# Splitting each 128x1024 weight tile with one cast and one subtraction in a decoder layer

## The chip, the cores and the metric

The kernel runs on one core of one Trainium2 chip. The metric is device time in microseconds (us) of one execution of the whole layer, as the median of several runs; lower is better.

## The reference

One decoder layer over 512 tokens with model width 2048: two gated token mixers side by side (latent attention and forgetting attention, 16 heads each), an output projection, then a product-key retrieval over 16384 single-neuron experts (8 heads, 16 experts a head and token). All of it is float32.

```python
h = rms_norm(x, mix_norm_g)
proj = einsum('bsd,de->bse', h, w_in)           # q, kv latents, fox q/k/v, forget, gates
...                                             # two causal attentions, y_a and y_b
merged = concatenate([y_a, y_b]) * sigmoid(gates + b_gate)
x = x + einsum('bse,ed->bsd', merged, w_out)
h2 = rms_norm(x, ffn_norm_g)
q = einsum('td,de->te', h2, w_peer_q)           # then scores, top-k of keys, top-k of pairs, softmax
a = einsum('td,thkd->thk', h2, u[experts])
x = x + einsum('thk,thkd->td', gates * gelu(a), v[experts])
```

## The kernel before

Every large product is made of three matmuls. A float32 operand is split into a rounded part `hi` (type float32r) and the rest `lo`; `mm3` (line 121) adds hi x hi, hi x lo and lo x hi. For a weight, `load` (line 92) brings a raw tile of 128 partitions x 1024 columns (512 KB) from memory on SP's queue; `half` (line 99) splits one half of it: a cast of 512 columns on ScalarE into `whi` and a subtraction on VectorE, or on GpSimd where `eng` says so, into `wlo` (`split`, line 87). So each raw tile costs two casts and two subtractions, and a tile `whi` with its tile `wlo` is called a pair here. Half a weight tile is called a unit or a half, a whole tile a whole.

The pools: phase 1 has NRAW = 3 raw tiles and 3 half pairs. Inside `spare(n, m)` (line 586) there is a second ring of n raw tiles and m half pairs; `load` counts all loads in `nraw` and takes the second ring when `nraw % nbuf >= NRAW`, with `nbuf` = NRAW + n. The output projection runs under `spare(NRAW2, NSP2)` = `spare(2, 3)`, the experts under `spare(1)`, that is one raw tile and two half pairs more.

The stages, in the order of time:

- Phase 1, the mixers (to about 1440 us). `col_tile` makes one 128x512 tile of the input projection from two raw tiles of `w_in`; `mla_pair` and `mla_head` use `w_up`. Attention work lies between them. There are 178 loads of w_in and 32 of w_up.
- Phase 2, the output projection (to about 1882 us). `merge` weaves a list of main units (`out_units`, tokens 0 to 511 in four blocks for q = 0, three blocks for q = 1) with a list of side units: `out0_units` finishes the first 128 tokens, `query0_units` makes their expert queries. Each main unit is 12 or 9 matmuls of 512 columns, each side unit 3. The first 14 main units stand alone; after that about 3.6 side units follow each main one. Odd halves of side tiles are subtracted on GpSimd. A unit is prepared (loaded, split) one place ahead of its use (LOOK = 1). After the merged list, q = 2 and 3 run alone, each with four groups (c) of four wholes (u).
- Phase 3, the queries of the other 384 tokens (`w_pq`), subtracted on GpSimd, with the top-k on VectorE, then the first 16 units of the expert rows (`up_stream`). Gathers of expert rows for the first tokens run from here on: `half` counts units and issues a gather on GpSimd's queue for every 400/128 units, whose product is a VectorE instruction of 2048 columns.
- Phase 4, the gate matrix (to about 2305 us; its order is written out by hand for TensorE, VectorE, ScalarE and GpSimd), with expert units between, and then the experts: `down` (`vt`) and `up_stream` (`ut`) in turn, 352 columns a matmul.

Outside the hand-ordered parts a planner orders each engine's instructions with a model of their times, by program order where several are ready, and gives out a buffer when its earlier tile has been released by all that used it.

Of the kernel before, what the change touches and what calls it, by code (L numbers as in the profile page):

```python
# [9 lines left out]
F32R = mybir.dt.float32r  # L10
# [9 lines left out]
P = 128  # L20
# [37 lines left out]
RC = 8  # L58
HALF = 512
RAWS = 3  # L60
NRAW = 3
NRAW2 = 2
NSP2 = 3
NC = 80
NU = 400
LAG = 28
# [10 lines left out]
class Kern:  # L77
# [18 lines left out]
        self.nc.sync.dma_start(raw[:, :n], src)  # L96
        return j, raw

    def half(self, w, i, eng=None):
        j, raw = w  # L100
        hi = self.wsp[j].tile([P, HALF], F32R, name="whi")
        lo = self.wsp[j].tile([P, HALF], F32R, name="wlo")
        ins = self.split(hi, lo, raw[:, i * HALF:(i + 1) * HALF], eng)
        self.last = lo
        if self.gathered is not None and not self.paused:
            self.units += 1
            if self.gathered < GATHERS and self.gathered * NU < self.units * PH * TOPK:
                with self.tc.issue_after(ins.ins):
                    self.gather(self.gathered)
                    self.gathered += 1  # L110
        return hi, lo

    def weight(self, src, n=1024, eng=None):
        w = self.load(src, n)
        return [self.half(w, i, eng) for i in range(n // HALF)]

    def cols(self, w, i, n):
        j, i = divmod(i, HALF)
# [86 lines left out]
    def col_tile(self, c):  # L205
        ps = self.mm.tile([P, SEQ], F32, name="mm")
        k = 0
        for u in range(2):
            w = self.early.pop((c, u), None) or self.load(self.a["w_in"][c, :, u])
            w = [self.half(w, i) for i in range(2)]  # L210
            for kt in range(8):
                self.mm3(ps, self.cols(w, kt * P, P), (self.hh[:, k], self.hlo[:, k]), k == 0, k == KD - 1)
                k += 1
        return ps
# [368 lines left out]
        return stack.enter_context(self.pool(name=name, bufs=1, side="right"))  # L583

    @contextlib.contextmanager
    def spare(self, n, m=2):
        with self.pool(name="wraw2", bufs=n) as wr, self.pool(name="wsp2", bufs=m) as ws:
            self.wraw.append(wr)
            self.wsp.append(ws)
            self.nbuf = NRAW + n  # L590
            yield
            self.nbuf = NRAW
            self.wraw.pop()
            self.wsp.pop()
# [22 lines left out]
    def piece(self, src, i, st, eng, run):  # L617
        def prep():
            if i == 0:
                st["w"] = self.load(src)  # L620
            return self.half(st["w"], i, eng)
        return prep, run

    def merged_half(self, q, i):
# [50 lines left out]
    def out0_units(self):  # L675
        st = {}
        m0 = self.right(self.low, "m0")
        mh = m0.tile([P, 24, P], F32R, name="m0h")
        ml = m0.tile([P, 24, P], F32R, name="m0l")
        raw = self.right(self.top, "m0r").tile([P, 24, P], F32, name="m0r")  # L680

        def unit(w, c, q, u, k2):
            if c == 0 and (u, k2) == (0, 0):
                qs = slice(q * 8 - 8, q * 8)
                self.nc.sync.dma_start(raw[:, qs], self.mrg[q * 8:q * 8 + 8, :, 0:P].rearrange("h p t -> p h t"))
                for k in range(q * 8 - 8, q * 8, 4):
                    self.split(mh[:, k:k + 4], ml[:, k:k + 4], raw[:, k:k + 4])
                if q == 3:
                    self.top.close()
            if (q, u, k2) == (1, 0, 0):  # L690
                st["ps"] = self.pa.tile([P, SEQ], F32, name="pa")
            k = (q - 1) * 8 + 2 * u + k2
            self.mm3(st["ps"], (mh[:, k], ml[:, k]), w, k == 0, k == 23)
            if k == 23:
                self.residual(st["ps"], 0, c, True)
                if c == 3:
                    self.low.close()
                    self.rows = self.right(self.low, "rows").tile([P, 3, D], F32, name="rows")
                    self.keys0 = self.rows[:, 2].rearrange("p (a b) -> p a b", b=NKEY)

        return [self.piece(self.a["w_out"][q, c, u], k2, st, self.nc.gpsimd if k2 else None,
                           lambda w, c=c, q=q, u=u, k2=k2: unit(w, c, q, u, k2))
                for c in range(4) for q in range(1, 4) for u in range(4) for k2 in range(2)]

# [9 lines left out]
    def query0_units(self, tk):  # L714
        nc = self.nc
        v = {}
        self.vals0 = tk.tile([P, 2, PH, TOPK], F32, name="vals0")
        self.ids0 = tk.tile([P, 2, PH, TOPK], U32, name="ids0")
        st = {}

        def norm():
            pool = self.right(self.top, "q0")
            v["hT"] = pool.tile([P, 2, KD, P], F32R, name="hT")
            v["qn"] = pool.tile([P, D], F32, name="qn")
            y = self.inv_rms(tk, range(1), "n0")
            for c in range(4):
                cs = slice(c * 512, c * 512 + 512)
                nc.vector.scalar_tensor_tensor(out=self.h0[:, cs], in0=self.x1[0][:, cs], scalar=y, in1=self.h0[:, cs],
                                               op0=OP.mult, op1=OP.mult)

        def turn(c):
            tp = self.pa.tile([P, 4, P], F32, name="pa")
            for i in range(4):
                k = 4 * c + i
                nc.tensor.transpose(tp[:, i], self.h0[:, k * P:k * P + P], self.ident)
            hT = v["hT"]
            self.split(hT[:, 0, 4 * c:4 * c + 4], hT[:, 1, 4 * c:4 * c + 4], tp)

        def query(w, c, k):
            if k == 0:  # L740
                st["ps"] = self.pa.tile([P, SEQ], F32, name="pa")
            self.mm3(st["ps"], (v["hT"][:, 0, k], v["hT"][:, 1, k]), w, k == 0, k == KD - 1)
            if k == KD - 1:
                nc.scalar.copy(v["qn"][:, c * 512:c * 512 + 512], st["ps"])

        def score(c):
            es = slice(4 * c, 4 * c + 4)
            qn = v["qn"]
            qT = self.rows[:, 0].rearrange("p (k t) -> p k t", t=P)
            sc = self.rows[:, 1].rearrange("p (k t) -> p k t", t=P)  # L750
            tp = self.pa.tile([P, 4, P], F32, name="pa")
            for i in range(4):
                nc.tensor.transpose(tp[:, i], qn[:, (4 * c + i) * P:(4 * c + i + 1) * P], self.ident)
            nc.scalar.copy(qT[:, es], tp)
            sp = self.pa.tile([P, 4, P], F32, name="pa")
            for i in range(4):
                nc.tensor.matmul(sp[:, i], qT[:, 4 * c + i], self.keys0[:, 4 * c + i], start=True, stop=True)
            nc.scalar.copy(sc[:, es], sp)
            for e in range(4 * c, 4 * c + 4):
                self.topk16(tk, self.vals0[:, e % 2, e // 2], self.ids0[:, e % 2, e // 2], sc[:, e], NKEY)  # L760

        bare = lambda f, *v: (lambda: None, lambda w: f(*v))
        out = [bare(norm)] + [None] * WAIT + [bare(turn, c) for c in range(4)]
        for c in range(4):
            out += [self.piece(self.a["w_pq"][c, k // 2], k % 2, st, nc.gpsimd if k % 2 else None,
                               lambda w, c=c, k=k: query(w, c, k)) for k in range(KD)]
            if c:
                out.insert(len(out) - KD + 4, bare(score, c - 1))
        return out + [bare(score, 3)]
# [59 lines left out]
    def phase3(self, hp):  # L829
        nc, a = self.nc, self.a  # L830
# [6 lines left out]
        with self.pool(name="tk", bufs=2) as tk, \  # L837
# [20 lines left out]
            for c in range(4):  # L858
# [1 line left out]
                ids = tk.tile([P, 2, ND, 2, TOPK], U32, name="ids")  # L860
                ps = [qp.tile([P, 512], F32, name="acc")[:, :TQ] for _ in range(4)]
                for u in range(8):
                    w = self.load(a["w_pq"][c, u])
                    for k2 in range(2):
                        k = 2 * u + k2
                        self.paused = c == 0 and k < 12
                        wh, wl = self.half(w, k2, nc.gpsimd)
                        for i in range(4):
                            es = slice(i * P, i * P + P)
                            self.mm3(ps[i], (wh[:, es], wl[:, es]), (self.dh[:, k], self.dl[:, k]), k == 0, k == KD - 1)  # L870
# [140 lines left out]
    def up_stream(self, rs, eng):  # L1011
        todo = [(r, u, i) for r in rs for u in range(2) for i in range(2)]
        raw = {}

        def fetch(r, u, i):
            if i == 0:
                raw[0] = self.load(self.a["ut"][r, u])
            return self.half(raw[0], i, eng)

        nxt = fetch(*todo[0])  # L1020
        for j, (r, u, i) in enumerate(todo):
# [5 lines left out]
            wh, wl = nxt  # L1027
            if j + 1 < len(todo):
                nxt = fetch(*todo[j + 1])
            for kt in range(4):  # L1030
                k = 8 * u + 4 * i + kt
# [99 lines left out]
    def build(self):  # L1131
        tc = self.tc
        with self.pool(name="cst", bufs=1) as cp, self.pool(name="dram", bufs=1, space=DRAM) as dp:
# [2 lines left out]
            self.xs = dp.tile([TQ, D], F32, name="xs")  # L1136
            self.hx = dp.tile([NX, D], F32, name="hx")
            self.aa = cp.tile([P, PH * TOPK], F32, name="aa")
            with self.pool(name="wraw", bufs=NRAW) as wr, self.pool(name="wsp", bufs=3) as ws:
                self.wraw, self.wsp = [wr], [ws]  # L1140
                self.phase1()
                with self.pool(name="res", bufs=1, side="right") as res:
# [98 lines left out]
```

## Time and profile before

| | us |
|---|---|
| median of 3 runs | 4241.0 |
| lowest and highest | 4234.29, 4250.6 |
| profiled execution | 4234.56 |
| its span, first to last instruction | 4232.8 |
| TensorE busy | 4095.4 (97%) |
| VectorE busy | 3083.4 (73%) |
| ScalarE busy | 1875.5 (44%) |
| GpSimd busy | 989.8 (23%) |

In the profile PE is TensorE's matmuls, PEld its weight loads, DVE VectorE, ACT ScalarE, POOL GpSimd and SP the queue that issues the loads. A matmul's record is about twice as long as the time to the next one's start, since they overlap; so TensorE's pace is read from starts or counts, not from the length of a record. "idle before" is the time that the engine stood still ahead of a group's instructions, with what ended it.

### The profile page before, as it was taken

What the parts mean: (1) busy time and instruction counts of PE and PEld (TensorE: products, weight loads), DVE (VectorE), ACT (ScalarE), POOL (GpSimd) and SP (SyncE); (2) the same over time, 40 slices, a digit from 0 to 9 for tenths busy, and PEclk for the clock granted to TensorE, in tenths of its full rate; (3) what the DMA queues carried; (4) which work ended last, traced back from release to release, by engine and by line L of the source; (5) the groups of instructions that cost most, each with busy time, mean ns of one, the idle gap of its engine ahead of it and who ended that gap; (6) DMA issues with size and microseconds to landing.
All of it is one profiled execution on the core that took longest, in us unless ns stands there. A gap on an engine that the chain in (4) does not pass through costs nothing.

```text
span 4232.8 us, 61035 instructions
## 1 busy us (share of the span) xinstructions
PE 4095.4 (97%) x22599; PEld 3734.9 (88%) x22599; DVE 3083.4 (73%) x5031; ACT 1875.5 (44%) x3584; POOL 989.8 (23%) x772
## 2 busy tenths in 40 slices
PE   8999999999999999998778999999999999999999
PEld 6878888888888777788778999999999999999998
DVE  8656556556655556868999878887878888888864
ACT  4555455555555455433266333333333333333332
POOL 1111111111101044227777111111111222221100
PEclk9999999999999999999899999999999999999999
DMA  4222222222222477665447888889888888988864
GB/s 135 88 80 80 79 86 85 78 82 90 78 85 83 146 245 243 202 268 204 151 143 225 340 306 330 323 326 325 318 310 315 319 320 326 333 328 322 314 222 145
DMA packets 245419, 896.81 MB, mean 212 GB/s; under 512 B 22816, under 2 KB 74016, under 8 KB 200992
## 3 DMA queue, kind: packets, MB, share of 16 engines
q1 hardware_dynamic: 190624, 540.47, 37.5%
q0 software_dynamic: 46272, 336.61, 21.5%
q10 hardware_dynamic: 8224, 15.82, 1.2%
q8 instruction: 177, 2.90, 0.3%
q14 instruction: 122, 1.00, 0.1%
HBM read 853.73 MB, written 39.06 MB: 211 GB/s over the span
## 4 chain that ended last, share of the span: by engine, by line
PE 85%; DVE 9%; issue 2%; DMA 2%; ACT 1%; POOL 1%; ACTq 0%; SPq 0%; DVEq 0%; POOLq 0%
PE acc L124 10%; PE acc L126 9%; PE acc L125 9%; PE mm L124 9%; PE mm L125 9%; PE mm L126 9%; PE a L126 7%; PE a L124 7%; PE a L125 7%; PE S L271 2%; DVE o L985 1%; DVE o L986 1%; DVE rows L915 1%; DMA raw<-w_out 1%; PE T L292 1%
## 5 line engine op out<-in xcount | busy, mean ns | idle before, releaser
L89 ACT CAST whi<-raw 128x512 fp32r<-128x512 f32 x1788 | 1097.9, 621 | 1808.0 <-PE acc L125 650.0
L90 DVE TENSOR_TENSOR wlo<-raw,whi 128x512 fp32r<-128x512 f32 x1596 | 1112.7, 709 | 652.6 <-ACT whi L89 622.4
L125 PE MATMUL acc<-Wl,whi 128*128 128x352 f32 x2048 | 660.1, 323 | 0.0
L124 PE MATMUL acc<-Wh,whi 128*128 128x352 f32 x2048 | 659.1, 324 | 0.5 <-ACT whi L89 0.5
L124 PE MATMUL a<-dh,whi 128*128 128x352 f32 x2016 | 657.0, 326 | 0.5 <-ACT whi L89 0.5
L126 PE MATMUL a<-dh,wlo 128*128 128x352 f32 x2016 | 648.8, 325 | 8.5 <-POOL wlo L90 8.0
L125 PE MATMUL a<-dl,whi 128*128 128x352 f32 x2016 | 654.1, 324 | 0.0
L126 PE MATMUL acc<-Wh,wlo 128*128 128x352 f32 x2048 | 627.1, 324 | 1.5 <-DVE wlo L90 1.5
L124 PE MATMUL mm<-hh,whi 128*128 128x512 f32 x1424 | 565.2, 397 | 8.7 <-ACT hh L526 8.7
L125 PE MATMUL mm<-hl,whi 128*128 128x512 f32 x1424 | 564.2, 396 | 6.4 <-DVE hl L527 6.3
L126 PE MATMUL mm<-hh,wlo 128*128 128x512 f32 x1424 | 562.1, 395 | 0.0
L126 PEld LDWEIGHTS a<-dh,wlo 128*128 128x128 f32 x2016 | 378.1, 188 | 10.1 <-POOL wlo L90 8.8
L124 PEld LDWEIGHTS acc<-Wh,whi 128*128 128x128 f32 x2048 | 384.5, 188 | 2.3 <-ACT whi L89 1.0
L125 PEld LDWEIGHTS acc<-Wl,whi 128*128 128x128 f32 x2048 | 385.2, 188 | 0.0
L126 PEld LDWEIGHTS acc<-Wh,wlo 128*128 128x128 f32 x2048 | 379.1, 188 | 3.2 <-DVE wlo L90 3.0
L124 PEld LDWEIGHTS a<-dh,whi 128*128 128x128 f32 x2016 | 379.3, 188 | 1.0 <-ACT whi L89 1.0
L125 PEld LDWEIGHTS a<-dl,whi 128*128 128x128 f32 x2016 | 379.3, 188 | 0.0
L90 POOL TENSOR_TENSOR wlo<-raw,whi 128x512 fp32r<-128x512 f32 x192 | 281.4, 1477 | 289.6 <-ACT whi L89 281.8
L125 PEld LDWEIGHTS mm<-hl,whi 128*128 128x128 f32 x1424 | 268.8, 189 | 65.8 <-DVE hl L527 11.5
L124 PEld LDWEIGHTS mm<-hh,whi 128*128 128x128 f32 x1424 | 269.5, 189 | 62.6 <-ACT hh L526 8.7
L126 PEld LDWEIGHTS mm<-hh,wlo 128*128 128x128 f32 x1424 | 269.0, 189 | 54.5 <-issue 0.2
L915 DVE CUSTOM_DVE_ANT_0 rows<-rows,h 128x2048 f32<-128x2048 f32 x128 | 300.3, 2347 | 6.7 <-DMA rows<-u,eidx 6.7
(374 smaller groups left out, 6431.9 us busy)
## 6 DMA issues: line engine op xcount, KB each, us to landing
raw<-ut SPq DMA_DIRECT2D x256, 512.0 KB, 5.3
raw<-vt SPq DMA_DIRECT2D x256, 512.0 KB, 6.1
raw<-w_in SPq DMA_DIRECT2D x178, 512.0 KB, 3.7
raw<-w_out SPq DMA_DIRECT2D x112, 512.0 KB, 4.6
raw<-w_pq SPq DMA_DIRECT2D x64, 512.0 KB, 4.3
gd<-rows SPq DMA_DIRECT2D x22, 1024.0 KB, 5.8
G<-gd SPq DMA_DIRECT2D x15, 1408.0 KB, 9.8
raw<-w_up SPq DMA_DIRECT2D x24, 512.0 KB, 3.6
```

Source lines behind the costliest of these rows:

```text
L89: nc.scalar.copy(hi, src)
L90: return (eng or nc.vector).tensor_tensor(out=lo, in0=src, in1=hi.bitcast(F32), op=OP.subtract)
L124: nc.tensor.matmul(out, wh, xh, start=start, stop=False)
L125: nc.tensor.matmul(out, wh, xl, start=False, stop=False)
L126: nc.tensor.matmul(out, wl, xh, start=False, stop=stop)
L271: nc.tensor.matmul(ps[:, :w], q[:, tb], k[:, :w], start=first, stop=False)
L292: nc.tensor.transpose(tp[:, (i - j) * P:(i - j + 1) * P], Ps[i][:, j * P:j * P + P], self.ident)
L915: nc.vector.tensor_tensor_reduce(out=row, in0=row, in1=self.h0, scale=1.0, scalar=0.0, op0=OP.mult, op1=OP.add, accum_out=self.aa[:, k:k + 1])
L985: nc.vector.tensor_tensor(out=o1, in0=lists[:, 0, t0:t0 + 4, None].to_broadcast(bc), in1=it, op=OP.is_equal)
L986: nc.vector.tensor_tensor(out=o2, in0=lists[:, 1, t0:t0 + 4, None].to_broadcast(bc), in1=it, op=OP.is_equal)
```

## The change

`half` becomes `whole`: one pair of 1024 columns, one cast and one subtraction per raw tile. A tile of 512 columns uses half of a wide pair. Callers that split half by half take both halves from the first call. Where odd halves went to GpSimd, odd tiles do. The count of units for the gathers goes up by two per tile, and at most one gather is issued per call.

The pools, in columns of pairs: 3 x 512 become 2 x 1024 in the first ring; in the output projection's second ring 3 x 512 become 1 x 1024; in the experts' 2 x 512 become 1 x 1024. Raw tiles: 3 become 2 in the first ring; the second rings keep 2 and 1.

```diff
-NRAW = 3
+NRAW = 2
 NRAW2 = 2
-NSP2 = 3
+NSP2 = 1
...
-    def half(self, w, i, eng=None):
+    def whole(self, w, n=1024, eng=None):
         j, raw = w
-        hi = self.wsp[j].tile([P, HALF], F32R, name="whi")
-        lo = self.wsp[j].tile([P, HALF], F32R, name="wlo")
-        ins = self.split(hi, lo, raw[:, i * HALF:(i + 1) * HALF], eng)
+        hi = self.wsp[j].tile([P, 1024], F32R, name="whi")
+        lo = self.wsp[j].tile([P, 1024], F32R, name="wlo")
+        ins = self.split(hi[:, :n], lo[:, :n], raw[:, :n], eng)
         self.last = lo
         if self.gathered is not None and not self.paused:
-            self.units += 1
+            self.units += n // HALF
...
-        return hi, lo
+        return [(hi[:, i:i + HALF], lo[:, i:i + HALF]) for i in range(0, n, HALF)]
 
     def weight(self, src, n=1024, eng=None):
-        w = self.load(src, n)
-        return [self.half(w, i, eng) for i in range(n // HALF)]
+        return self.whole(self.load(src, n), n, eng)
...
-            w = [self.half(w, i) for i in range(2)]
+            w = self.whole(w)
...
-    def spare(self, n, m=2):
+    def spare(self, n, m=1):
...
     def piece(self, src, i, st, eng, run):
         def prep():
             if i == 0:
-                st["w"] = self.load(src)
-            return self.half(st["w"], i, eng)
+                st["w"] = self.weight(src, eng=eng)
+            return st["w"][i]
...
-        return [self.piece(self.a["w_out"][q, c, u], k2, st, self.nc.gpsimd if k2 else None,
+        return [self.piece(self.a["w_out"][q, c, u], k2, st, self.nc.gpsimd if u % 2 else None,
...
-            out += [self.piece(self.a["w_pq"][c, k // 2], k % 2, st, nc.gpsimd if k % 2 else None,
+            out += [self.piece(self.a["w_pq"][c, k // 2], k % 2, st, nc.gpsimd if k // 2 % 2 else None,
...
-                    w = self.load(a["w_pq"][c, u])
+                    self.paused = c == 0 and u < 6
+                    w = self.weight(a["w_pq"][c, u], eng=nc.gpsimd)
                     for k2 in range(2):
                         k = 2 * u + k2
-                        self.paused = c == 0 and k < 12
-                        wh, wl = self.half(w, k2, nc.gpsimd)
+                        wh, wl = w[k2]
...
             if i == 0:
-                raw[0] = self.load(self.a["ut"][r, u])
-            return self.half(raw[0], i, eng)
+                raw[0] = self.weight(self.a["ut"][r, u], eng=eng)
+            return raw[0][i]
...
-            with self.pool(name="wraw", bufs=NRAW) as wr, self.pool(name="wsp", bufs=3) as ws:
+            with self.pool(name="wraw", bufs=NRAW) as wr, self.pool(name="wsp", bufs=2) as ws:
```

## Rows read from the trace of the kernel before

**Rows 1.** The page's busy times: us, share of the span, instructions.
```profile
PE 4095.4 (97%) x22599; PEld 3734.9 (88%) x22599; DVE 3083.4 (73%) x5031; ACT 1875.5 (44%) x3584; POOL 989.8 (23%) x772
```

**Rows 2.** By stage: length, busy PE, PEld, DVE, ACT, POOL (count); clock, DMA share, GB/s.
```profile
25.00:1440.00 1415.00, 1408.54 (x6801) 1159.08 (x6800) 859.82 (x1610) 760.71 (x1508) 175.44 (x125) 0.99 0.27 85
...
1490.00:1745.00 255.00, 241.23 (x1032) 189.37 (x1031) 159.84 (x295) 137.88 (x250) 107.15 (x77) 0.99 0.75 245
1745.00:1882.00 137.00, 130.89 (x574) 106.24 (x572) 111.02 (x233) 48.77 (x96) 26.23 (x16) 1.00 0.65 240
1882.00:1940.00 58.00, 55.03 (x318) 52.83 (x319) 31.05 (x78) 22.30 (x43) 28.57 (x22) 0.94 0.50 173
1940.00:2130.00 190.00, 143.05 (x797) 138.87 (x795) 187.60 (x651) 51.08 (x101) 142.45 (x82) 0.87 0.49 168
2130.00:2305.00 175.00, 145.01 (x1044) 138.70 (x1045) 170.89 (x174) 117.42 (x298) 144.34 (x138) 0.98 0.58 172
2305.00:4200.00 1895.00, 1891.47 (x11669) 1884.25 (x11668) 1507.00 (x1908) 697.39 (x1222) 347.57 (x298) 1.00 0.85 311
```

**Rows 3.** Groups of instructions: shape and count, then busy us, mean ns, idle before.
```profile
L90 DVE TENSOR_TENSOR wlo<-raw,whi 128x512 fp32r<-128x512 f32 x1596 | 1112.7, 709 | 652.6 <-ACT whi L89 622.4 <-PE y L126 11.4 <-PE mm L125 4.3
L89 ACT CAST whi<-raw 128x512 fp32r<-128x512 f32 x1788 | 1097.9, 621 | 1808.0 <-PE acc L125 650.0 <-PE a L125 478.5 <-PE mm L125 315.4
...
L928 DVE SCALAR_TENSOR_TENSOR x<-rows,aa,x 128x2048 f32<-128x2048 f32 x128 | 300.3, 2346 | 0.0
...
L90 POOL TENSOR_TENSOR wlo<-raw,whi 128x512 fp32r<-128x512 f32 x192 | 281.4, 1477 | 289.6 <-ACT whi L89 281.8 <-PE acc L126 5.0 <-POOL wlo L90 1.9
...
L89 ACT CAST Wh<-w 128x352 fp32r<-128x352 f32 x128 | 61.8, 484 | 22.6 <-DVE w L1054 21.7 <-PE acc L126 0.5
```

**Rows 4.** 2305 to 4200 us: the casts' group, and raw's landing times.
```profile
L89 ACT CAST whi<-raw 128x512 fp32r<-128x512 f32 x971 | 600.7, 621 | 1170.6 <-PE acc L125 573.9 <-PE a L125 475.0 <-DMA raw<-vt 38.0
...
DMA to landing us min/median/max: 3.4/5.8/16.5
```

**Rows 5.** The chain that ended last, 1535 to 1625 us: start, us, what.
```profile
1585.59 6.64 DMA raw<-w_out
...
1597.05 6.20 DMA raw<-w_out
```

**Rows 6.** Timeline of PE: start, us, instruction; first and last of thirteen.
```profile
1584.70 0.40 PE L126 MATMUL pa<-whi,m0l 128*128 128x512 f32 x1
...
1587.51 0.39 PE L126 MATMUL pa<-whi,m0l 128*128 128x512 f32 x1
```

**Rows 7.** 1490 to 1745 us: subtractions' ns min/median/max, landing, VectorE's group.
```profile
L90 DVE TENSOR_TENSOR wlo<-raw,whi x131: 666/693/1794, 1489.9 to 1741.7; 128x512 fp32r<-128x512 f32 x131
L90 POOL TENSOR_TENSOR wlo<-raw,whi x77: 1262/1297/2078, 1491.5 to 1734.9; 128x512 fp32r<-128x512 f32 x77
...
DMA to landing us min/median/max: 3.4/4.4/8.4
...
L90 DVE TENSOR_TENSOR wlo<-raw,whi 128x512 fp32r<-128x512 f32 x131 | 111.3, 870 | 81.0 <-ACT whi L89 76.9 <-POOL wlo L90 3.7
```

**Rows 8.** Timeline of DVE and of POOL from 1593 us.
```profile
1593.95 4.76 DVE L90 TENSOR_TENSOR wlo<-raw,whi 128x512 fp32r<-128x512 f32 x3 [0.17 <-ACT whi L89]
...
1593.47 2.99 POOL L90 TENSOR_TENSOR wlo<-raw,whi 128x512 fp32r<-128x512 f32 x2 [3.01 <-ACT whi L89]
```

**Rows 9.** 1745 to 1882 us: the casts' waits, and the gather products' group.
```profile
ACT whi L89 <- PE acc L126: 67.5, 47, 3.5
...
L915 DVE CUSTOM_DVE_ANT_0 rows<-rows,h 128x2048 f32<-128x2048 f32 x12 | 27.4, 2286 | 0.7 <-DMA rows<-u,eidx 0.6
```

**Rows 10.** 1882 to 1960 us: GpSimd's groups.
```profile
L90 POOL TENSOR_TENSOR wlo<-raw,whi 128x512 fp32r<-128x512 f32 x29 | 43.2, 1501 | 35.3 <-ACT whi L89 30.1 <-PE acc L126 5.0
L913 POOL DMA_INDIRECT rows<-u,eidx x6 | 5.7, 958 | 0.9 <-DVE ids L778 0.2 <-PE acc L126 0.2
```

**Rows 11.** 25 to 1440 us: raw's landing times.
```profile
DMA to landing us min/median/max: 2.6/3.7/6.9
```

## The prediction, made before the changed kernel was timed

> **What bounds the kernel now.** I read the busy times first: TensorE is busy 97% of 4232.8 us, VectorE 73%, ScalarE 44% [rows 1]. That says only which engine to fear for, so the next view is busy time stage by stage [rows 2]. Up to 1440 us (mixers) TensorE idles 6.5 of 1415 us, from 2305 to 4200 us (expert matmuls) 3.5 of 1895. From 1940 to 2305 us VectorE is the full one (187.6 of 190, then 170.9 of 175) and TensorE waits for top-k and the gate matrix. Between them lies the output projection, 1490 to 1745 us, where TensorE idles 13.8 of 255 and no engine is full.
>
> Then the splits themselves [rows 3]: a cast of 512 columns takes 621 ns, a subtraction 709 ns on VectorE, 1477 ns on GpSimd. None of it is on the path where TensorE is full: in the expert stage the casts idled 573.9 and 475.0 us waiting for TensorE to give back a pair [rows 4]. So cheaper splits buy nothing there; what can change the time is how early a pair and a raw tile come free. The chain of waits shows where that is tight already: around 1590 us it runs through DMA waits of 6.64 and 6.20 us for w_out [rows 5].
>
> **The price of a wide split.** Cast: 484 ns at 352 columns, 621 at 512, so 0.86 ns a column and 621 + 512 x 0.86 = 1.06 us at 1024. VectorE: 709 ns at 512, 2346 at 2048 [rows 3], so 709 + 512 x 1.07 = 1.25 us. GpSimd has no wider row of this form: between 1.3 us (its median now, no gain from more columns counted) and 2 x 1.3 = 2.6 us [rows 7]; I take 2.5, near the upper end, because the work doubles. A whole on VectorE thus saves 1.24 - 1.06 = 0.18 us of ScalarE and 1.42 - 1.25 = 0.17 of VectorE, on engines that wait anyway, but its first matmul waits 1.06 + 1.25 = 2.31 us (GpSimd: 3.56) where the half's waited 1.3 (1.9).
>
> **Mixers, 25 to 1440 us.** Three half pairs become two whole pairs, three raw tiles two. A whole feeds 24 matmuls; at 0.234 us a 512-column matmul (twelve steps in 2.81 us [rows 6]) that is 5.6 us. A pair given back is split again in 2.3 us plus queueing, while TensorE has the other whole for 5.6. A raw tile is held for 3.7 us of landing [rows 11] plus 2.3, and two serve 11.2 us of TensorE. Covered; some splits queue behind attention work. I take +4 (0 to 25).
>
> **Output projection, 1490 to 1745 us.** The term that decides. Here the four raw tiles and three pairs are two rings: load n goes to the second when n mod 4 is 2 or 3, and this ring now has one pair (before: three halves). 210 loads stand before the stage (178 of w_in, 32 of w_up), and the merged list of units gives 112 more. Counted through the list, 56 fall to the single pair: 4 main wholes before the side units begin, then 11 main (4 of four blocks, 7 of three) and 41 side wholes, 20 of them subtracted on VectorE and 21 on GpSimd. Two neighbouring loads share that pair, so the second is not cast before TensorE has finished the first. Occupancy of one load is cast + subtraction + matmuls + 0.2 us of hand-overs (an estimate from the 0.17 us between cast and subtraction in [rows 8]):
> - side, VectorE: 1.06 + 1.25 + 6 x 0.234 + 0.2 = 3.9 us, x20 = 78
> - side, GpSimd: 1.06 + 2.5 + 1.4 + 0.2 = 5.2, x21 = 108
> - main, four blocks: 2.5 + 24 x 0.234 = 8.1, x4 = 32; three blocks: 2.5 + 18 x 0.234 = 6.7, x7 = 47
>
> Together 265 us, against 255 that the stage takes now: the single pair alone is a longer chain than the stage. That is the floor, +10, with TensorE ready whenever a split is. Two things come on top. TensorE is in order and is often inside another whole's half (2.1 to 2.8 us) when the pair is ready: I take 0.75 us for each of 52 loads, +39. And the subtractions hold each other up: VectorE's mean here is 870 ns against a median of 693 [rows 7], and three of them took 4.76 us while two of GpSimd's ran [rows 8]. That is 0.18 us for a half; with twice the length of both, 0.35 us x 52 = +18. Sum 322, so +67. The ceiling is no overlap at all: 241 us of TensorE plus 52 uncovered splits (31 x 2.31 + 21 x 3.56 = 146), +132. Raw tiles are not the limit: 4.4 us of landing [rows 7] plus 2.3 to 3.6 for four tiles, where a load is wanted every 255 / 105 = 2.4 us.
>
> The Trainium skill's page "SBUF — State Buffer", section "Who interferes with whom", says that a VectorE instruction with two SBUF inputs and a GpSimd one that reads SBUF block each other for the whole instruction. [rows 8] agree: 4.76 us where 2.1 were due. By that rule the excess doubles with the width (the +18); were it the same per instruction, it would be 52 x 0.18 = +9.
>
> The seven main wholes before 1490 us hold two such pairs of neighbours: +4 (0 to 6).
>
> **Output projection, last half, 1745 to 1882 us.** 32 wholes in eight groups of four. 210 + 112 = 322, so each group's first two wholes share the single pair, and the units of one accumulator go in order: TensorE finishes the first, then waits for 2.31 + 0.2 us. The first product needs only whi, and three blocks of it (0.7 us) can go early: 1.8 us. The subtraction can find VectorE inside a 2.29 us gather product or a select step; VectorE is busy 111 of 137 us [rows 2, 9], so +1.2. 8 x 3.0 = +24 (8 x 1.8 = 14 to 8 x 4.8 = 38; zero if the planner moves another group's work in). The 47 waits of casts for TensorE that stand there now [rows 9] are the spare time that goes.
>
> **Queries, 1882 to 1940 us, and the VectorE-bound stretch to 2305.** Two pairs, subtraction on GpSimd: a whole is ready 3.76 us after its pair; TensorE has the other for 24 x 0.18 = 4.4 us (318 matmuls in 58 us [rows 2]). Just covered, unless one of the 0.96 us gather issues stands first on GpSimd [rows 10]. +6 (0 to 20). From 1940 on VectorE carries no weight split, so its time stays: 0 (-6 to +10, GpSimd's longer blocks ahead of the gate matrix's products). Behind each GpSimd subtraction gather issues and those products queue; who waits is VectorE, and then TensorE.
>
> **Experts, 2305 to 4200 us.** Rings merge to three whole pairs and three raw tiles (before five halves, four tiles). TensorE takes 24 x 0.162 = 3.9 us a whole (11669 matmuls in 1895 us [rows 2]), so a split has 7.8 us to be ready, more than before. A raw tile is held 5.8 us of landing [rows 4] + 2.31 + up to 2.35 behind a gather product [rows 3] = 10.5 us when it meets one, against 3 x 3.9 = 11.7. +3 (0 to 30). Gather issues keep their rate: two units are counted at once and at most 0.64 of a gather falls due. The start (third load now waits for the first split): 0 (-2 to +4).
>
> **Sum.** 4 + 67 + 4 + 24 + 6 + 0 + 3 = +108. On the profiled execution's 4234.6 us that is 4342.6; the median of the runs is 6.4 higher, so 4349, +2.5%.
>
> **Rivals.**
> 1. No slower: the single pair does not decide, because the planner fills each wait with the other stream's work. TensorE has 13.8 us of idle time there to begin with, and main and side sums are independent. It holds if the hold per load of the single pair stays under 255 / 52 = 4.9 us; then only stray waits stay, about +5: 4246. Against it: the 265 us floor holds for any order of that ring. This is also the case in which the change does nothing that can be measured.
> 2. Much slower: raw tiles starve the experts. Landing goes up to 16.5 us [rows 4]; it decides once a hold averages more than 11.7 us; at 12.5 each of some 485 wholes (971 halves [rows 4]) waits (12.5 - 11.7) / 3 = 0.27 us, +131 beside the forecast: 4480. For it: one tile fewer at 311 GB/s [rows 2]. Against: fewer loads in flight also land sooner, and pairs give 7.8 us of slack.
> 3. Faster: fewer, wider instructions free VectorE and GpSimd where they are full. At most the 13.8 us in the projection, the 6.1 behind it, and 14 wholes x 0.4 in the gate stage go: -25, 4216. Against: on the stretch where VectorE is full the weight splits are GpSimd's.
>
> "Perfetto Trace Analysis" of the Trainium skill, "Optimizing Scalar/DVE Operations", has both sides: grouping helps where the engine is saturated (rival 3), and where it is not but causes bubbles elsewhere, breaking instructions up lets work finish sooner (the forecast). [rows 2] put the stage with the most splits per matmul on the second side, VectorE at 160 of 255 us.
>
> **How the numbers follow.** Forecast 0.65, rival 1 0.19, rival 2 0.08, rival 3 0.08. The forecast's own range is 4275 to 4430: from lows (10 + 14 and 10 for the rest, on 4241) to highs (132 + 38 + 19). To hold 8 in 10 the range takes in rival 1 and stops before 2 and 3: 4238 to 4440. A measurement of this kernel tells about 0.5% (21 us) from no change. Faster by more: rival 3's share, 0.06. Within: rival 1 and the near ends of the others, 0.22. Slower: 0.72.
>
> **What would show it.** Right: casts of 1.06 us, subtractions of 1.25 and 2.5; the first stage that is longer is 1490 to 1745, by about 67 us, its TensorE idle time under waits for wlo or whi, those casts waiting for TensorE's last product of the load before; eight gaps of some 3 us in the last half of the projection; the expert stage within 10 us of its 1895. Wrong: a projection stage of 255 to 265 us (rival 1), casts of the expert stage waiting for DMA (rival 2), or mixers longer by more than 25 us, which would say that two whole pairs are too few there.

## The result, and the profile after

The changed kernel takes 4351.4 us (median of 4 runs, 4343.45 to 4352.33) against 4239.2 us for the kernel before beside it: a ratio of 1.0264, 95% interval 1.0248 to 1.0279, so 112 us slower. The prediction had said 4349, and slower. The profiled executions have spans of 4350.1 and 4232.8 us, 117.3 us apart.

The page of the changed kernel, its busy times and the groups of the weight splits (shape and count, busy us, mean ns of one, idle before), to be laid beside [rows 1] and [rows 3]:

```profile
PE 4140.4 (95%) x22599; PEld 3761.9 (86%) x22599; DVE 2978.3 (68%) x4237; ACT 1730.8 (40%) x2694; POOL 940.8 (22%) x676
...
L89 ACT CAST whi<-raw 128x1024 fp32r<-128x1024 f32 (+1 forms) x898 | 938.5, 1047 | 1852.1 <-PE acc L124 576.0
L90 DVE TENSOR_TENSOR wlo<-raw,whi 128x1024 fp32r<-128x1024 f32 x802 | 986.6, 1232 | 693.9 <-ACT whi L89 689.4
...
L90 POOL TENSOR_TENSOR wlo<-raw,whi 128x1024 fp32r<-128x1024 f32 x96 | 244.9, 2557 | 396.5 <-ACT whi L89 390.1
```

The change did what it says: ScalarE is busy 145 us less, VectorE 105 us less, GpSimd 49 us less. TensorE, with the same 22599 matmuls, is busy 45 us more. That is the first odd number of this page, and the stages show where it comes from (columns as in [rows 2]: length, busy PE, PEld, DVE, ACT, POOL; clock, DMA share, GB/s):

```profile
1499.00:1827.00 328.00, 270.35 (x1037) 205.06 (x1036) 134.56 (x230) 126.85 (x146) 94.69 (x40) 0.90 0.59 188
1827.00:1985.00 158.00, 140.44 (x588) 111.03 (x587) 109.72 (x201) 42.27 (x58) 19.25 (x14) 0.96 0.58 202
1985.00:2235.00 250.00, 199.53 (x1109) 192.11 (x1109) 212.45 (x730) 68.44 (x108) 158.75 (x64) 0.91 0.51 176
2235.00:2430.00 195.00, 159.52 (x1050) 155.12 (x1049) 169.01 (x176) 118.86 (x291) 138.31 (x125) 0.88 0.53 155
2430.00:4317.00 1887.00, 1881.05 (x11664) 1875.64 (x11664) 1464.05 (x1423) 613.75 (x736) 326.66 (x296) 1.00 0.86 312
```

The projection's stretch with side units, where TensorE was busy 241.23 of 255 us at a clock of 0.99 [rows 2], is 328 us long now, with 270.35 us busy at 0.90. To compare the kernels exactly I cut every trace at the same instructions: the start of the first main matmul of the projection, the last query matmul of the side units ("first part"), the last main matmul ("last half"), the first comparison of the gate matrix ("queries"), its last matmul ("gate"), the last expert matmul. In us:

| | mixers | first part | last half | queries | gate | experts | median |
|---|---|---|---|---|---|---|---|
| before | 1437.0 | 300.4 | 140.6 | 248.1 | 178.2 | 1916.5 | 4239.2 |
| after | 1439.7 | 386.9 | 157.9 | 250.3 | 194.8 | 1909.0 | 4351.4 |
| e1_even | 1443.1 | 316.6 | 132.2 | 244.5 | 192.8 | 1909.8 | 4252.3 |
| e2_four | 1441.3 | 325.9 | 137.9 | 246.2 | 192.7 | 1909.6 | 4269.8 |
| e3_narrow | 1451.8 | 350.6 | 150.5 | 258.9 | 196.8 | 1915.2 | 4345.6 |
| e4_ring2 | 1438.7 | 312.2 | 138.4 | 252.0 | 178.1 | 1917.3 | 4252.5 |
| e5_even_dve | 1443.4 | 297.3 | 135.2 | 242.3 | 193.0 | 1908.4 | 4237.2 |
| e6_even_lazy | 1441.2 | 319.9 | 132.1 | 251.7 | 178.2 | 1903.3 | 4228.8 |
| e7_even_dve_lazy | 1441.7 | 298.6 | 135.2 | 240.5 | 178.2 | 1898.9 | 4212.3 |
| e8_before_dve | 1437.5 | 296.7 | 139.5 | 252.8 | 178.2 | 1924.1 | 4236.2 |

The stages are those of one profiled execution each; it lies 11 and 6 us over the median in e6_even_lazy and e8_before_dve, and 9 and 6 us under it in e3_narrow and e7_even_dve_lazy. From before to after the first part grows by 86.5 us, the last half by 17.3, the gate by 16.6; the experts shrink by 7.5.

In the first part, the same cut in both kernels (columns as above):

```profile
1437.00:1737.40 300.40, 285.97 (x1227) 225.76 (x1225) 184.18 (x337) 155.90 (x284) 111.50 (x80) 0.98 0.73 236
```

and after:

```profile
1439.70:1826.60 386.90, 319.77 (x1227) 243.93 (x1225) 158.65 (x270) 145.18 (x176) 94.69 (x40) 0.89 0.58 185
```

Both hold 1227 matmuls. TensorE's idle time goes from 300.40 - 285.97 = 14.4 us to 386.90 - 319.77 = 67.1, that is +52.7; its busy time for the same matmuls goes up by 33.8 us, with the granted clock at 0.89 in place of 0.98. So there are two terms, and the prediction had priced one.

What TensorE and the casts wait for in that stretch (the view of waits of after, 1440 to 1830 us: us in total, times, longest):

```profile
ACT whi L89 <- PE pa L125: 88.7, 59, 6.0
ACT whi L89 <- PE acc L125: 67.6, 19, 9.7
...
PE pa L124 <- POOL wlo L90: 29.8, 20, 2.9
...
PE pa L123 <- ACT whi L89: 14.6, 14, 1.7
```

Casts wait for the last product (hi x lo's line, L125) of an earlier load to give the pair back, and TensorE waits for the split that follows. The chain of after around 1600 us (start, us, what) has this as one row of steps:

```profile
1599.36 1.05 ACT whi L89
...
1600.48 2.36 POOL wlo L90
...
1602.88 0.79 PE pa L124
1603.67 0.43 PE pa L125
...
1605.46 1.05 ACT whi L89
...
1606.54 1.24 DVE wlo L90
...
1607.82 0.79 PE pa L124
```

Cast, subtraction, matmuls, next cast, one after another: beside the 3.5 us of the first cast and subtraction TensorE has a single matmul to do, at 1600.46 in the timeline below. In [rows 5] this place was a chain of DMA waits. The second term stands in the matmuls themselves (timeline of TensorE in after: start, us, instruction, idle before and what ended it):

```profile
1597.84 0.50 PE L124 MATMUL pa<-wlo,m0h 128*128 128x512 f32 x1 [1.22 <-POOL wlo L90]
...
1598.65 0.39 PE L124 MATMUL pa<-wlo,m0h 128*128 128x512 f32 x1
1598.88 0.40 PE L125 MATMUL pa<-whi,m0l 128*128 128x512 f32 x1
1600.46 0.59 PE L123 MATMUL pa<-whi,m0h 128*128 128x512 f32 x1 [1.18 <-ACT whi L89]
1602.88 0.79 PE L124 MATMUL pa<-wlo,m0h 128*128 128x512 f32 x1 [1.84 <-POOL wlo L90]
1603.47 0.63 PE L125 MATMUL pa<-whi,m0l 128*128 128x512 f32 x1
1603.90 0.63 PE L123 MATMUL pa<-whi,m0h 128*128 128x512 f32 x1
1604.33 0.63 PE L124 MATMUL pa<-wlo,m0h 128*128 128x512 f32 x1
...
1610.97 0.39 PE L125 MATMUL pa<-whi,m0l 128*128 128x512 f32 x1
1611.20 0.39 PE L123 MATMUL pa<-whi,m0h 128*128 128x512 f32 x1
```

After the wait of 1.22 us the matmuls still start 0.23 us apart, as in [rows 6]. After the next one, of 1.18 us, the first matmul is already longer (0.59 us for 0.40), and behind the wait of 1.84 us they start 0.43 us apart, until 1610.97, where 0.23 is back. The granted clock is 1.00 over 1598 to 1600 us, 0.68 over 1600 to 1602, and 0.50 over 1602 to 1610, the lower of the two levels (1.2 of 2.4 GHz). So the clock had begun to fall before the longest of the three waits was over.

### The profile page after: what moved, and what is told of

Its sections match the earlier page's. It is cut to its first block, busy times and chain, and to the rows that moved or that the text cites. A ratio compares the mean times of both kernels' runs of the same rounds, so it can differ in the third digit from the quotient of the medians.

```text
span 4350.1 us, 58012 instructions
## 1 busy us (share of the span) xinstructions
PE 4140.4 (95%) x22599; PEld 3761.9 (86%) x22599; DVE 2978.3 (68%) x4237; ACT 1730.8 (40%) x2694; POOL 940.8 (22%) x676
## 4 chain that ended last, share of the span: by engine, by line
PE 84%; DVE 7%; POOL 3%; DMA 2%; issue 2%; ACT 2%; ACTq 0%; DVEq 0%; SPq 0%; POOLq 0%
PE acc L125 9%; PE acc L124 9%; PE acc L123 9%; PE mm L125 9%; PE mm L123 9%; PE mm L124 9%; PE a L125 7%; PE a L124 7%; PE a L123 7%; PE S L270 2%; POOL wlo L90 2%; ACT whi L89 1%; DVE wlo L90 1%; DVE rows L914 1%; DVE o L984 1%
## 5 line engine op out<-in xcount | busy, mean ns | idle before, releaser
L89 ACT CAST whi<-raw 128x1024 fp32r<-128x1024 f32 (+1 forms) x898 | 938.5, 1047 | 1852.1 <-PE acc L124 576.0
L90 DVE TENSOR_TENSOR wlo<-raw,whi 128x1024 fp32r<-128x1024 f32 x802 | 986.6, 1232 | 693.9 <-ACT whi L89 689.4
L125 PE MATMUL a<-dh,wlo 128*128 128x352 f32 x2016 | 657.4, 326 | 3.4 <-POOL wlo L90 3.4
L125 PE MATMUL acc<-Wh,wlo 128*128 128x352 f32 x2048 | 656.7, 323 | 1.2 <-DVE wlo L90 1.2
L125 PE MATMUL mm<-hh,wlo 128*128 128x512 f32 x1424 | 566.7, 398 | 1.9 <-DVE wlo L90 1.9
L125 PEld LDWEIGHTS a<-dh,wlo 128*128 128x128 f32 x2016 | 383.7, 190 | 4.2 <-POOL wlo L90 4.2
L125 PEld LDWEIGHTS acc<-Wh,wlo 128*128 128x128 f32 x2048 | 384.6, 188 | 2.4 <-DVE wlo L90 2.3
L90 POOL TENSOR_TENSOR wlo<-raw,whi 128x1024 fp32r<-128x1024 f32 x96 | 244.9, 2557 | 396.5 <-ACT whi L89 390.1
L125 PEld LDWEIGHTS mm<-hh,wlo 128*128 128x128 f32 x1424 | 269.5, 189 | 56.2 <-DVE wlo L90 2.6
```

Of the source, the lines that this page charges most:

```text
L89: nc.scalar.copy(hi, src)
L90: return (eng or nc.vector).tensor_tensor(out=lo, in0=src, in1=hi.bitcast(F32), op=OP.subtract)
L125: nc.tensor.matmul(out, wl, xh, start=False, stop=stop)
```

## The experiments

The theory: the time is lost because the second ring of the projection has one pair, and two of four loads share it. The rivals: the loss lies in the width of the instructions (a first matmul that waits 2.31 us or 3.56 in place of 1.3 or 1.9), or in there being fewer raw tiles and pairs at all.

### The pairs dealt evenly

Same pairs, raw tiles and instructions as after; only which pair a load takes is counted on its own, so that each of the three pairs gets every third load, while the raw tiles are dealt as before.

```diff
+NPAIR = 2
...
-        return j, raw
+        q = self.nraw % self.pbuf >= NPAIR
+        return q, raw
...
-            self.nbuf = NRAW + n
+            self.nbuf, self.pbuf = NRAW + n, NPAIR + m
...
```

> The changed kernel, but the wide pairs are dealt by a counter of their own: every third load takes the second ring's single pair, in place of two of every four. Four raw tiles, three wide pairs and all instructions stay. Theory (ring: two neighbouring loads share one pair): the sum of the holds, about 660 us, spreads over three pairs, 220 us each, which is under the 255 us of the stage; the stretch from the first main matmul to the last query matmul of the output projection (300.4 us before, 386.9 after the change) comes down to 310 to 335, its last half (140.6 before, 157.9 after) to 141 to 146, the kernel to 4260 to 4295. Rival (width: a wide split comes later and GpSimd and VectorE block each other longer): the first part stays above 365 and the kernel at 4335 or more.

Measured: 4252.3 us (4250.11 to 4255.46), ratio to before 1.0038 (1.0024 to 1.0053). The first part falls from 386.9 to 316.6 us:

```profile
1443.10:1759.70 316.60, 293.46 (x1247) 232.06 (x1246) 168.93 (x270) 145.73 (x177) 96.33 (x40) 0.97 0.70 228
```

Idle time is 23.1 us in place of 67.1, and the clock is back at 0.97. The last half falls from 157.9 to 132.2, below before's 140.6; the planner has 20 more matmuls in the first part here, some 5 us that the last half has less. So 99 of the 112 us were the dealing of the pairs, with not one instruction made narrower. The last half and the kernel came out lower than the theory expected (141 to 146, 4260 to 4295). What stays against before is +16 in the first part, +15 in the gate stage and +6 in the mixers, less 19 in the other three stages.

### One more pair, one raw tile fewer

On e1_even:

```diff
-NRAW2 = 2
-NSP2 = 1
+NRAW2 = 1
+NSP2 = 2
```

> The changed kernel with four wide pairs in the output projection, dealt evenly, and three raw tiles in place of four (the memory holds no more). Ring theory: another pair takes away what is left of the waits for pairs: first part 300 to 320 us, last half 141, kernel 4250 to 4280. Rival (raw tiles bind once pairs do not): a raw tile is held 4 us of landing and 2.3 to 3.6 us of splitting, so three give a load every 2.3 us at best where 2.4 is wanted; the first part is then no shorter than with three pairs and four raw tiles, 320 to 345.

Measured: 4269.8 us, ratio 1.0083 (1.0065 to 1.0101); first part 325.9, longer than with three pairs. It is what the rival expected (320 to 345). The casts' waits from 1490 to 1750 us say why, first e1_even (its casts stand in line 91, its subtractions in line 92, since lines were added above them):

```profile
ACT whi L91 <- PE pa L128: 45.9, 37, 6.4
ACT whi L91 <- PE acc L128: 37.4, 19, 3.8
ACT whi L91 <- DMA raw<-w_out: 15.7, 12, 2.5
```

then e2_four:

```profile
ACT whi L91 <- DMA raw<-w_out: 74.8, 48, 6.4
ACT whi L91 <- DMA raw<-w_pq: 27.9, 17, 4.7
```

With four pairs and three raw tiles the casts wait little for TensorE (15.6 us in 11 waits) and mostly for loads: a raw tile is held through its landing and both instructions of its split, and three are too few here. For four pairs beside four raw tiles the memory has no room. Whether a fourth pair by itself would help stays open.

### Narrow instructions in the wide pools

On after: the pairs and rings of after, but each whole is split by two casts and two subtractions of 512 columns.

```diff
-        ins = self.split(hi[:, :n], lo[:, :n], raw[:, :n], eng)
+        for i in range(0, n, HALF):
+            ins = self.split(hi[:, i:i + HALF], lo[:, i:i + HALF], raw[:, i:i + HALF], eng)
```

> The changed kernel's pools and rings, but each tile is split by two casts and two subtractions of 512 columns into the halves of the wide pair. Ring theory: the first part keeps most of its loss, since the pair is held as before and only the first half's matmuls start about 1 us (VectorE) to 1.7 us (GpSimd) earlier: 355 to 380 us of 386.9; the last half 150 to 158. Width theory: the first part comes back to 300 to 325. For the gate matrix (178.2 us before, 194.8 after the change): if GpSimd's wide subtractions block the products there, it comes back to 176 to 183, else it stays near 195. For the experts (1916.5 before, 1909.0 after): if the number of splits sets TensorE's pace there, it goes back to 1914 or more. Kernel 4300 to 4340 by the ring theory, 4240 to 4270 by the width theory.

Measured: 4345.6 us, ratio 1.0262 (1.0243 to 1.028): as slow as after, within 6 us, and above both ranges that were expected. The first part is 350.6 us, just under the expected stretch and 36 less than after's:

```profile
1451.80:1802.40 350.60, 305.85 (x1226) 231.00 (x1225) 166.78 (x339) 154.22 (x287) 104.07 (x80) 0.95 0.64 205
```

So the width does count where a pair is short: with halves, TensorE starts on the first half while the second is split (around 1650 us a first half's second product starts at 1651.65, while GpSimd subtracts the second half until 1652.83). But it is 36 of the 86 us there, and the mixers (+12), the queries (+9) and the experts (+6) take most of it back; why they do was not traced further. The width alone is not the reason for the loss.

### The smaller ring alone

On before, halves and all, only the second ring of the projection has two half pairs in place of three.

```diff
-NSP2 = 3
+NSP2 = 2
```

> The kernel before with one part of the change alone: the second ring of the output projection has two half pairs (the bytes of one wide pair) in place of three; all else stays narrow. Ring theory: a smaller ring costs by itself, but half pairs come back after half a tile: first part 310 to 335 us (300.4 before), last half 141 to 146, kernel 4250 to 4275. Width theory: nothing changes, 4240.

Measured: 4252.5 us, ratio 1.0039 (1.0022 to 1.0056); the first part 312.2 against 300.4, and the other stages within 4 us of before. The ring's size costs 12 us without any widening, as the ring theory expected. That is the same memory as one wide pair; with a whole in it, a ring of one cannot split ahead at all, where two halves still can.

### GpSimd's side subtractions moved to VectorE

On e1_even, VectorE subtracts all side wholes:

```diff
-        return [self.piece(self.a["w_out"][q, c, u], k2, st, self.nc.gpsimd if u % 2 else None,
+        return [self.piece(self.a["w_out"][q, c, u], k2, st, None,
...
-            out += [self.piece(self.a["w_pq"][c, k // 2], k % 2, st, nc.gpsimd if k // 2 % 2 else None,
+            out += [self.piece(self.a["w_pq"][c, k // 2], k % 2, st, None,
```

> e1_even (wide pairs dealt evenly) with the side tiles of the output projection all subtracted on VectorE, none on GpSimd. If a GpSimd subtraction of 2.4 us still lies in the hold of a pair, 40 of 105 loads come 1.2 us earlier and the mutual blocking ends: the first part goes from 316.6 to 300 to 312 us, the kernel from 4252 to 4238 to 4248. Rival: TensorE now waits for main wholes and raw tiles, or VectorE (169 of 317 us busy, 220 then) queues more: 316 or longer.

Measured: 4237.2 us, ratio 1.0004 (0.9994 to 1.0013): level with before, 15 us below e1_even. The first part is 297.3 us, 19 less than e1_even's and 3 less than before's, both just under what was expected. VectorE's and GpSimd's groups in that part from 1490 us on, e1_even:

```profile
L92 DVE TENSOR_TENSOR wlo<-raw,whi 128x1024 fp32r<-128x1024 f32 x68 | 98.4, 1461 | 96.9 <-ACT whi L91 96.4
...
L92 POOL TENSOR_TENSOR wlo<-raw,whi 128x1024 fp32r<-128x1024 f32 x40 | 96.3, 2409 | 220.8 <-ACT whi L91 144.6 <-DVE x L600 58.2 <-DVE h L730 12.6
```

and e5_even_dve:

```profile
L92 DVE TENSOR_TENSOR wlo<-raw,whi 128x1024 fp32r<-128x1024 f32 x107 | 128.8, 1221 | 63.3 <-ACT whi L91 62.8
```

One whole subtracted on GpSimd costs its pair 2.41 us, on VectorE 1.22; and the 68 on VectorE took 1.461 us in the mean while GpSimd worked too, 1.221 once it did not. By these means 40 wholes should be ready some 1.2 us earlier and 68 some 0.24 us earlier. The Trainium skill's page "SBUF — State Buffer", section "Who interferes with whom", says that the two engines share a port pair and hold each other up; the two means agree with it.

### Half by half again in the gate stage

On e1_even, only where expert rows are subtracted on GpSimd (the rows ahead of the experts and those between the products of the gate matrix): wide pairs as before, but each half is cast and subtracted when its own half is asked for.

```diff
...
-                raw[0] = self.weight(self.a["ut"][r, u], eng=eng)
-            return raw[0][i]
+                j, w = self.load(self.a["ut"][r, u])
+                raw[0] = [self.wsp[j].tile([P, 1024], F32R, name=n) for n in ("whi", "wlo")] + [w]
+            hi, lo, w = [t[:, i * HALF:i * HALF + HALF] for t in raw[0]]
+            self.split(hi, lo, w, eng)
+            return hi, lo
```

> e1_even, but in the hand-ordered stretch of the gate matrix and the expert rows ahead of it each half of a wide pair is cast and subtracted on GpSimd just before its unit, as before the change, in place of both halves at once. Theory (burst): two subtractions in a row on GpSimd, 2.4 to 3.3 us, delay the products of the gate matrix that stand behind them by program order, and TensorE waits for those; spread over two units they fit: the gate stretch goes from 192.8 to 176 to 182 us, the kernel from 4252 to 4235 to 4242. Rival (two pairs or two raw tiles in place of three are what is missing there): it stays at 190 or more.

Measured: 4228.8 us, ratio 0.9979 (0.997 to 0.9989), 23 us below e1_even and 6 below the range of the theory. The gate stage is 178.2 us as in before, which gives 14.6 of the 23. What TensorE waits for in it, before:

```profile
PE acc L1003 <- POOL o L989: 23.5, 21, 1.4
```

after:

```profile
PE acc L1002 <- POOL o L988: 32.6, 14, 2.9
```

and e6_even_lazy:

```profile
PE acc L1005 <- POOL o L991: 23.9, 21, 1.4
```

In after, fewer waits, but longer ones: a whole split in one go puts one block of 2.4 to 2.9 us on GpSimd ahead of products that stand in a hand-written order, where a half took 1.3 to 1.7. The timeline of GpSimd in after:

```profile
2268.14 2.91 POOL L90 TENSOR_TENSOR wlo<-raw,whi 128x1024 fp32r<-128x1024 f32 x1 [1.05 <-ACT whi L89]
2271.01 3.10 POOL L988 TENSOR_TENSOR o<-o,lists 128x256 f32<-128x256 f32 x3
```

and in e3_narrow, whose gate stage is as long as after's (196.8):

```profile
2295.48 3.33 POOL L90 TENSOR_TENSOR wlo<-raw,whi 128x512 fp32r<-128x512 f32 x2 [0.63 <-ACT whi L89]
2298.77 3.10 POOL L989 TENSOR_TENSOR o<-o,lists 128x256 f32<-128x256 f32 x3
```

Two narrow subtractions in one block do the same as one wide: three products are late together. e6_even_lazy, with the same two narrow subtractions spread over two units, does not. So it is the burst and not the width. And again most of the price is the clock. The gate stage cut at the same instructions, before (columns as above):

```profile
2126.00:2304.30 178.30, 146.35 (x1048) 139.24 (x1048) 172.80 (x177) 118.44 (x304) 145.25 (x138) 0.97 0.57 167
```

and after:

```profile
2234.80:2429.60 194.80, 159.32 (x1049) 154.91 (x1047) 169.21 (x176) 118.73 (x290) 137.91 (x125) 0.88 0.53 155
```

TensorE idles 3.5 us more (32.0 to 35.5) and is busy 13.0 us longer with the same matmuls.

### Both together

> Both edits of e5_even_dve and e6_even_lazy in one kernel. If the two add up: 4252 - 16 - 8 = 4228, 10 us under the kernel before (4239), from the experts' stretch (6.7 us shorter with wide splits) and the last half of the projection (8 us shorter in e1_even). If the first part does not gain from VectorE alone: 4236 to 4245, no difference from the kernel before.

It has the edits of e5_even_dve and of e6_even_lazy. Measured: 4212.3 us (4206.57 to 4222.54), ratio to before 0.9948 (0.9933 to 0.9963): 0.5% faster than the kernel before, and 16 us under the 4228 expected from adding the two edits up. By the table: first part 298.6, last half 135.2, queries 240.5, gate 178.2, and the experts 1898.9 against before's 1916.5, the largest single gain. That stage in the windows' view:

```profile
2294.20:4193.00 1898.80, 1894.38 (x11806) 1888.95 (x11805) 1473.64 (x1436) 617.83 (x740) 331.83 (x298) 1.00 0.86 312
```

TensorE idles 4.4 us in it, and its clock is the full one: what it gained against before is the pace of the matmuls, of which more below.

### The same move on the kernel before

On before, the side halves of GpSimd go to VectorE:

```diff
-        return [self.piece(self.a["w_out"][q, c, u], k2, st, self.nc.gpsimd if k2 else None,
+        return [self.piece(self.a["w_out"][q, c, u], k2, st, None,
...
-            out += [self.piece(self.a["w_pq"][c, k // 2], k % 2, st, nc.gpsimd if k % 2 else None,
+            out += [self.piece(self.a["w_pq"][c, k // 2], k % 2, st, None,
```

> The kernel before (half splits, its pools) with the side tiles of the output projection all subtracted on VectorE. It tells whether e7_even_dve_lazy owes its gain over the kernel before to wide splits or to taking GpSimd off the side tiles. If a GpSimd subtraction in the hold of a pair costs there too (1.4 against 0.87 us a half, with mutual blocking): first part 285 to 295 us from 300.4, kernel 4224 to 4234, and about half of e7's gain is this move. If half pairs had slack enough (six of them): 298 to 302, kernel 4238.

Measured: 4236.2 us against 4235.1 beside it, ratio 0.9995 (0.998 to 1.001): no difference in the kernel, as expected from slack; the first part, 296.7 us, lies between the two ranges. With halves dealt over six pairs GpSimd's subtractions were covered. So what e7_even_dve_lazy wins is not that move by itself.

## Why the prediction was right

Its reason for the sign and the place held: the single pair of the second ring. e1_even moves nothing but the dealing of pairs and takes 99 of 112 us back. By its steps:

| step | predicted, us | measured |
|---|---|---|
| cast, subtraction on VectorE, on GpSimd | 1.06, 1.25, 2.5 | 1.05, 1.23, 2.56 |
| mixers | +4 | +2.7 |
| first part (+67, and +4 for the seven wholes) | +71 | +86.5 |
| last half | +24 | +17.3 |
| queries (+6, and 0 for where VectorE is full) | +6 | +2.2 |
| gate | 0 | +16.6 |
| experts | +3 | -7.5 |
| sum | +108 | +117.8 (spans: +117.3) |

**The first part** came out near its size for a reason only half foreseen. The sum priced waits alone, +71; the idle time grew by 52.7. The mutual blocking (+18) was too large: VectorE's mean in after's first part, from 1490 us on, is 1325 ns over a median of 1226, 0.10 us for each of 64 subtractions and 6 in all, against 0.35 for each of 52. In e1_even, where more of the splits lie side by side, the excess is 0.24. That explains some 12 of the 18 us; the rest would lie in TensorE not being ready (+39), which was not measured by itself. What the sum lacked is the 33.8 us by which the same 1227 matmuls ran longer at a clock of 0.89. [rows 2] had a sign of it: 0.87 in the stretch where TensorE was busy 143.05 of 190 us. Too large by 18 and short by 34, the total was nearer than its parts, and that is luck; so is a sum within 10 us of the spans, in which the gate stage's miss and the experts' partly cancel.

**The last half** has the eight gaps, but seven are shorter than forecast. TensorE's waits of after, 1827 to 1985 us:

```profile
PE acc L124 <- DVE wlo L90: 8.8, 7, 5.9
PE acc L123 <- ACT whi L89: 8.8, 8, 1.2
```

Eight waits for whi and seven for wlo, 17.6 us in all or 2.2 a group. The mean hides that one group waits 7.0 us (1.13 for whi and then the 5.91 for wlo, while VectorE was in the selection for the first tokens, two reductions of 2.27 us in it); the other seven wait 0.7 to 2.2, 1.5 in the mean, near the 1.8 that the sum had before VectorE's share. I had 3.0, and the 5.2 us of idle time that stood there before (140.6 long, 135.4 busy) should have been taken off: idle +12.4, and +4.9 of busy time at a clock of 0.96.

**The gate stage** is the step that failed. I named the longer blocks on GpSimd ahead of the gate matrix's products and put them at 0 (-6 to +10), since VectorE carried no weight split there. The work on the engines did stay; what changed is that three products come late at once, TensorE's waits go from at most 1.4 us to 2.9, and the clock falls to 0.88. e6_even_lazy, which undoes only this on e1_even, takes the stage back to 178.2.

**The experts** were to lose 3 us by waits. TensorE's windows from the end of the gate matrix on, before:

```profile
2304.40:4232.00 1927.60, 1914.47 (x11818) 1906.96 (x11816) 1518.86 (x1928) 702.56 (x1230) 347.57 (x298) 1.00 0.84 308
```

after:

```profile
2429.70:4350.00 1920.30, 1904.61 (x11818) 1898.89 (x11816) 1476.79 (x1440) 617.03 (x739) 326.96 (x296) 1.00 0.85 309
```

Idle time grew by 2.6 us (13.1 to 15.7), close to the +3; but the same 11818 matmuls were busy 9.9 us less, which no step had. e3_narrow, with the pools of after and the instructions of before, is between (1911.5 busy).

**The rivals.** Rival 1 (the planner fills the waits) fell with the first part. What it describes, waits that the other work covers, is e1_even: 4252 against its 4246. Rival 2 (raw tiles starve the experts) did not come: landing there is 3.3/5.7/16.4 us, as in [rows 4], and casts do wait longer for raw tiles of vt, 109.6 us in 31 waits against 38.0 in [rows 4], but TensorE's idle time grew by only 2.6 us. It did come in e2_four, in the projection, with one raw tile fewer. Rival 3 (faster by fewer instructions) is not in this kernel, but something of it is in e7_even_dve_lazy, 0.5% under before, and not where I looked for it: its largest gain is in the experts.

## What to carry to other kernels

When buffers are made larger and fewer, count how the loads are dealt over them, ring by ring: two of four loads on a single buffer made a serial chain of cast, subtraction and matmul, though three buffers were there for the same loads, and a few lines that deal them evenly gave back 99 of 112 us. Then price a new wait of TensorE twice, once as idle time and once as the slower clock of the matmuls behind it. And a wider instruction did no harm here where buffers gave it slack, but it did ahead of another engine's work in a hand-written order, where the burst counted even with each instruction narrow.

## What the runs showed of the hardware

In after's projection the granted clock fell to 1.2 GHz (0.50 over 1602 to 1610 us) behind waits of 1.22 and 1.18 us with five matmuls between them. Over the whole first part it was 0.89, and the same matmuls were busy 33.8 us longer, beside 52.7 us of added waits; in the gate stage 13 us beside 3.5. The Trainium skill's page "TensorE: Matmul & The Clock Gate", section "HAM oscillation — how this bites in real kernels", tells of a loop in which each tile's wait sends the clock down again; this trace agrees that the clock falls at waits, here with shorter and irregular ones.

The pace of TensorE in the expert stage differs between kernels at a granted clock of 1.00 throughout. The four kernels with 512-column splits take 1915 to 1924 us there, the six with wide ones 1899 to 1910, and nearly all of the difference is busy time of the same matmuls. e6_even_lazy and e7_even_dve_lazy, whose code for that stage is that of e1_even, are a further 6 to 11 us shorter; the gathers of the first kind that fall into the stage are 98 in before, after, e1_even and these two, so it is not their number. Each figure is of one trace, but the medians agree: e5_even_dve and e7_even_dve_lazy, which differ by that one edit, lie 24.9 us apart, and the gate stage gives 14.8 of them. What links these kernels to the pace was not settled: it goes with the number of split instructions beside the matmuls in the first case, and in the second I have no measurement that explains it.
